# Product-key stage: the second parts of slabs, subkeys and query weights subtracted on VectorE instead of GpSimd

## Chip, cores and metric

One core of one Trainium2 chip. The metric is the device time of one execution in microseconds (us), the median of several runs. Engines are named as the profile names them: PE is TensorE (matmuls), PEld its weight loads, DVE is VectorE, ACT is ScalarE, POOL is GpSimd, SP is SyncE, which here only issues DMAs.

## What is computed

Two transformer blocks over 512 tokens of width 1024. The first has a latent attention, an indexed sparse attention and a mixture of experts; the second has three kinds of attention and then a product-key layer. All in float32. The change touches the product-key layer alone (and the slab products that are done ahead of it):

```python
def peer_ffn(h, w_q, subkeys, u, v):              # h: 512 tokens x 1024, already normed
    q = (hf @ w_q).reshape(T, 8, 2, 128)           # 8 heads, two halves of a key
    sc = jnp.einsum('thpd,hpkd->thpk', q, subkeys) # 128 scores per half
    s1, i1 = lax.top_k(sc[:, :, 0], 16)
    s2, i2 = lax.top_k(sc[:, :, 1], 16)
    # the 16 best sums s1 + s2 of each head choose 16 of 128 * 128 = 16384 experts
    top_s, pos = lax.top_k(cand, 16)
    gate = jax.nn.softmax(top_s, axis=-1)
    act = gelu(einsum('chkd,cd->chk', u[idx], h))  # a row of u and one of v for each expert
    out = einsum('chk,chkd->cd', gate * act, v[idx])
```

## The kernel before

**Two parts.** TensorE multiplies in a 32 bit format (fp32r) that drops low bits, so each operand is split: the first part is the rounded value, written by ACT (L185, `nc.scalar.copy`), the second is the rest, source minus first part (L187). `mm3` (L178 to L180) then takes three products in place of one. `split` puts the subtraction on DVE unless its argument `le` names another engine; `wunit` (L203) fetches a raw unit of 128x1024 values, splits it, and hands `le` on. In the tile names, `wr` is a raw unit, `wh` and `wl` are its two parts, and there are three buffers of each part and ten raw ones in this stage (`ring(10)`, L1761, nw=3).

**The product-key stage.** The matrix u is cut into 128 slabs of 128 experts. For 384 of the 512 tokens, `peer_s` (L1424) takes dense products of a slab with the normed tokens `hp` (24 matmuls of 128x384, then a gelu); for the first 128 tokens the rows of the chosen experts are gathered by indirect DMAs, which POOL issues (L1564), and DVE takes their dot products (L1569, tile `hy`) and later adds rows of v (L1567). In the order of the code:

- `peer_norm` (L1401) and `peer_early` (L1412), at the end of the stage before: norms, their transposes and splits (`hp`), and the products of slabs 0 and 1 (`ehl`).
- the subkeys (`sk`, two units) and the query weights (four chunks of four units, L1476): q, scores `s` and, on DVE, the 16 best of each half (`top16`, L1622 to L1626).
- `choose` for each of four tiles of 128 tokens, nearly all on DVE: the best sums and their keys, with five loops over 8 heads on 128x256 values (`big`, L1672, L1673, L1674, L1679, L1680) and three reductions (L1675, L1676, L1681). For tiles 1 to 3 PE then transposes the lists (L271, `t<-ident,i`).
- the matrix of gates: one-hot matrices on DVE (`ohA`, `ohB`, `ohE`, L1522 to L1525), multiplied on PE (L1530, L1531), copied by ACT into `stg`, stored and loaded again as `G`.
- slabs 2 to 71 (`s_step`, L1457, called at L1584), with one gather every second slab from the 24th on; then the main loop (L1592 on) over 128 slabs of v, 18 matmuls of 128x512 each, with the 56 slabs of u that are left (72 to 127) done eight steps ahead, and gathers at 1.3 a step.

**Order.** The engines run their queues in the order in which the program was laid down. That order isn't the order of the code: a planner (`schedule_with_timeline_sim`, L1852) lays it down when the program is built, from what it takes each instruction to last. So slabs run on PE beside the query, `choose` and the one-hot work, and a gather's dot product stands in DVE's queue in the midst of `choose`.

Of the kernel before, what the change touches and what calls it, by code (L numbers as in the profile page):

```python
# [20 lines left out]
P = 128  # L21
NT = 4
D = 1024
# [22 lines left out]
def staged(n, lag, first, then):  # L46
    """then(i, first(i)) for all i, first() running `lag` ahead"""
    r = {}
    for i in range(n + lag):
        if i < n:  # L50
            r[i] = first(i)
        if i >= lag:
            then(i - lag, r.pop(i - lag))


class Fill:
    """products kept in DRAM until the merge: sigmoids of gate columns, and output projections times those; 128
    columns at a time, feature-major.  They are queued in small pieces behind others whose results the tensor engine
    would wait for"""
# [7 lines left out]
    def gates(self, w, X, n0, n1, bias=None, raw=False):  # L67
        """gt[i] = tanh(z / 2) for the column tiles i = n0 .. n1 - 1 of z = (x @ W)^T + 2 bias; sigmoid(z) =
        (1 + tanh(z / 2)) / 2.  Without tanh and bias if raw"""
# [11 lines left out]
    def outs(self, w, X, g0, dst, prev=None, bias=None, raw=False):  # L81
        """dst[i] = 2 sigmoid(gate g0 + i) * (x @ W)^T of column tile i, + prev[i]"""
        nk = X[0].shape[1]
# [31 lines left out]
    def step(self, pool, after, n, end=False):  # L115
        """n row tiles, behind the instruction `after`; or those of the units that have begun (end)"""
# [23 lines left out]
    def rest(self, pool):  # L140
        """whatever is left"""
        while self.cur is not None or self.nxt is not None or self.jobs:
            self.step(pool, None, 1)


class Kernel:
# [12 lines left out]
    def ring(self, nr, nw=3):  # L159
        """the rings of weights: nr raw units as they arrive, nw units split into two parts"""  # L160
# [42 lines left out]
    def wunit(self, ap, nk, n, le=None, w=None, pool=None, after=None, cut=1):  # L203
        """one unit of weights: nk row tiles of n columns, split into two fp32r parts, in `cut` steps"""
# [9 lines left out]
    def proj_tok(self, XH, XL, units, nk, n, evac, nt=NT, cols=None, raws=(), le=None):  # L214
        """rows = tokens: psum[t] = x[t] @ W, W in units of row tiles"""
# [16 lines left out]
    def proj_tok1(self, XH, XL, units, nk, n, evac, follow=None, order=range(NT), pool=None):  # L232
        """proj_tok with all units on chip first: the tiles of tokens finish one after another; follow(t) comes behind
        the products of the next tile"""
# [16 lines left out]
    def proj_feat(self, XH, XL, units, nk, n, evac, ntok=512, le=None):  # L251
        """rows = output features: psum[c] = (x @ W[:, c])^T"""
# [15 lines left out]
    def T(self, out, src):  # L268
        """exact transpose"""
# [3 lines left out]
    def units(self, name, j, kn=2):  # L273
        """chunk j of a weight laid out [chunk, unit, partition, kn * n]"""
# [3 lines left out]
    def rstd(self, ss, n, pool=None, bufs=3):  # L278
        """1 / sqrt(ss / n + eps): first guess from the exponent bits, three Newton steps"""
# [26 lines left out]
    def to_feat(self, y, H, L, g=None, pool=None):  # L306
        """H, L [128, 8, 128] = parts of the transpose of y [128, 1024], times g [128, 8, 1]"""
# [16 lines left out]
    def norm_T(self, pool, src, g, HT=None, LT=None, nt=NT, keep=None):  # L324
        """rmsnorm(src(t)) * g into keep(t) if given, and the parts of its transpose into HT, LT [128, 8, nt * 128];
        src(t) -> [128, 1024]"""
# [11 lines left out]
    def rope(self, dst, src, nh, half, C, S):  # L338
        """dst, src [128, nh, >=2*half]; C = [c|c], S = [-s|s] of [128, 2*half]"""
# [10 lines left out]
    def transp(self, srcs, m, H, L, scale=None):  # L350
        """H, L [m, len(srcs) * 128] = parts of the transposes of srcs ([128, m] each)"""
# [5 lines left out]
    def softmax_rows(self, pool, s, n, bias=None, chunk_mask=False, np=NP):  # L357
        """P = softmax of the rows of psum s[:, :n]"""
# [21 lines left out]
    def block1_mix(self, cx, cm):  # L380
        nc, a = self.nc, self.a
        with ExitStack() as c0:
# [30 lines left out]
            with ExitStack() as c2:  # L413
# [5 lines left out]
                # keys for heads in the lower and upper 64 rows, zeros in the others: whole columns keep the clock up  # L419
# [74 lines left out]
                # latent attention  # L494
# [33 lines left out]
            with ExitStack() as c2:  # L528
# [6 lines left out]
                def behind(h, ins):  # L535
                    # the selection is needed later: one tile of queries per head
# [22 lines left out]
            # sparse attention  # L559
# [32 lines left out]
            # gated merge and output projection  # L592
# [1263 lines left out]
```

## Time and profile before

| | us |
|---|---|
| median of 3 runs | 2906.74 (2906.39 to 2907.47) |
| span of the profiled execution | 2904.9 |
| busy in that span: PE | 2735.4 (94%) |
| DVE | 2110.4 (73%) |
| ACT | 1283.6 (44%) |
| POOL | 1135.7 (39%) |

The span lies 1.84 us under the median of the runs. Shares over the whole span are means over stages; the product-key stage takes up about the last 1345 us. PE's busy time is modelled, and a matmul's record lasts longer than the distance to the next one, so the pace of matmuls is read from the distance between their starts.

### The profile page before, as it was taken

The numbers are of one execution on the slowest core, as the hardware profiler recorded it, in microseconds if no ns is written. First come the engines' busy times: TensorE is split into PE (matmuls) and PEld (weight loads), VectorE is DVE, ScalarE is ACT, GpSimd is POOL, SyncE is SP. The second block draws the span as 40 slices with busy tenths as digits, with TensorE's granted clock in tenths as the row PEclk, the third lists the DMA queues.
The fourth block names the chain that finished last, engine by engine and source line by source line (L and its number), as shares of the span: only waits on it lengthen the run. The fifth ranks groups of instructions, "written<-read, shape, count | busy, mean of one in ns | idle before, by whom it ended". The sixth has DMA issues, their size and how long they took to land.

```text
span 2904.9 us, 38412 instructions
## 1 busy us (share of the span) xinstructions
PE 2735.4 (94%) x13674; PEld 2353.4 (81%) x13674; DVE 2110.4 (73%) x4017; ACT 1283.6 (44%) x2021; POOL 1135.7 (39%) x682
## 2 busy tenths in 40 slices
PE   6999999789888999999998997899999999999999
PEld 5877777666666878798977897889988888888887
DVE  5758765798778464544475699999977788788885
ACT  3553443466665464533343232346643333333332
POOL 1120110465552231210122344554446565657661
PEclk9999999899999999999999998999999999999999
DMA  7222236688884332221353234567699999999994
GB/s 189 69 77 80 77 130 243 217 294 314 287 315 146 112 120 77 79 76 55 97 194 133 84 122 143 177 201 252 232 322 330 359 323 346 336 345 338 338 332 157
DMA packets 226774, 589.40 MB, mean 203 GB/s; under 512 B 25616, under 2 KB 90384, under 8 KB 224912
## 3 DMA queue, kind: packets, MB, share of 16 engines
q1 hardware_dynamic: 187408, 444.23, 44.3%
q0 software_dynamic: 39168, 142.65, 14.2%
q8 instruction: 110, 1.80, 0.2%
q14 instruction: 88, 0.72, 0.1%
HBM read 521.76 MB, written 65.04 MB: 202 GB/s over the span
## 4 chain that ended last, share of the span: by engine, by line
PE 62%; DVE 12%; issue 3%; POOL 2%; DMA 2%; ACT 1%; SPq 0%; POOLq 0%; DVEq 0%; ACTq 0%
PE acc L178 13%; PE acc L179 13%; PE acc L180 12%; PE s L178 4%; PE s L179 4%; PE s L180 4%; PE t L178 3%; PE t L180 3%; PE t L179 3%; DVE wl L187 2%; PE t L271 1%; DVE big L1672 1%; POOL wl L187 1%; DVE big L1680 1%; PE s L1530 1%
## 5 line engine op out<-in xcount | busy, mean ns | idle before, releaser
L187 POOL TENSOR_TENSOR wl<-wr,wh 128x1024 fp32r<-128x1024 f32 (+1 forms) x290 | 682.3, 2359 | 1139.0 <-ACT wh L185 1081.0
L185 ACT CAST wh<-wr 128x1024 fp32r<-128x1024 f32 (+3 forms) x637 | 622.3, 991 | 656.1 <-issue 298.9
L187 DVE TENSOR_TENSOR wl<-wr,wh 128x1024 fp32r<-128x1024 f32 (+3 forms) x347 | 493.1, 1428 | 181.8 <-ACT wh L185 177.9
L180 PE MATMUL acc<-hp,wl 128*128 128x384 f32 (+1 forms) x688 | 248.3, 361 | 6.4 <-POOL wl L187 6.4
L178 PE MATMUL acc<-hp,wh 128*128 128x384 f32 (+1 forms) x688 | 247.6, 361 | 0.0
L179 PE MATMUL acc<-hp,wh 128*128 128x384 f32 (+1 forms) x688 | 247.3, 359 | 0.0
L1564 POOL DMA_INDIRECT wr<-in_peer_u,idx x128 | 165.7, 1295 | 174.2 <-DVE dot L1569 59.2
L1564 POOL DMA_INDIRECT wr<-in_peer_v,idx x128 | 167.7, 1310 | 137.7 <-DVE x L1567 50.8
L1567 DVE SCALAR_TENSOR_TENSOR x<-wr,dot,x 128x1024 f32<-128x1024 f32 x128 | 195.7, 1529 | 26.3 <-DMA wr<-in_peer_v,idx 25.6
L185 ACT CAST WH<-act 128x384 fp32r<-128x384 f32 x128 | 65.8, 515 | 324.7 <-PE s L179 309.8
L1569 DVE CUSTOM_DVE_ANT_0 hy<-wr,gbc 128x1024 f32<-128x1024 f32 x128 | 184.4, 1440 | 23.4 <-DMA wr<-in_peer_u,idx 22.9
L179 PE MATMUL acc<-wl,WH 128*128 128x512 f32 x512 | 200.3, 391 | 0.0
L178 PE MATMUL acc<-wh,WH 128*128 128x512 f32 x512 | 197.4, 392 | 2.1 <-ACT WH L185 2.1
L180 PE MATMUL acc<-wh,WL 128*128 128x512 f32 x512 | 198.4, 389 | 0.0
L178 PE MATMUL t<-hp,wh 128*128 128x384 f32 x448 | 152.2, 340 | 0.0
L180 PE MATMUL t<-hp,wl 128*128 128x384 f32 x448 | 151.1, 337 | 0.8 <-POOL wl L187 0.8
L179 PE MATMUL t<-hp,wh 128*128 128x384 f32 x448 | 150.8, 337 | 0.0
L180 PEld LDWEIGHTS acc<-hp,wl 128*128 128x128 f32 x688 | 134.6, 196 | 11.9 <-POOL wl L187 6.8
L179 PEld LDWEIGHTS acc<-hp,wh 128*128 128x128 f32 x688 | 134.4, 195 | 5.3
L178 PEld LDWEIGHTS acc<-hp,wh 128*128 128x128 f32 x688 | 134.7, 196 | 4.8
L179 PE MATMUL s<-wl,XT 128*128 128x512 f32 x256 | 107.9, 421 | 27.3 <-DVE wl L187 24.8
L178 PEld LDWEIGHTS acc<-wh,WH 128*128 128x128 f32 x512 | 96.4, 188 | 20.5 <-ACT WH L185 2.4
(648 smaller groups left out, 7168.0 us busy)
## 6 DMA issues: line engine op xcount, KB each, us to landing
wr<-in_peer_vL SPq DMA_DIRECT2D x128, 512.0 KB
wr<-in_peer_uT SPq DMA_DIRECT2D x126, 512.0 KB
wr<-in_w_gu SPq DMA_DIRECT2D x122, 512.0 KB
wr<-in_w_dn SPq DMA_DIRECT2D x62, 512.0 KB
gd<-stg SPq DMA_DIRECT2D x12, 2048.0 KB
G<-gd SPq DMA_DIRECT2D x32, 768.0 KB
wr<-in_w_gate SPq DMA_DIRECT2D x24, 512.0 KB
act<-ad SPq DMA_DIRECT2D x56, 192.0 KB
```

Of the source, the lines that this page charges most:

```text
L178: mm(out, lh, rh, start=start, stop=False)
L179: mm(out, lh, rl, start=False, stop=False)
L180: return mm(out, ll, rh, start=False, stop=stop)
L185: nc.scalar.copy(H, src)
L187: return (le or nc.vector).tensor_tensor(L, src, H.bitcast(F32), op=ALU.subtract)
L271: self.nc.tensor.transpose(out, src, self.ident[:k, :k])
L1530: nc.tensor.matmul(o, A[:, b, :, ti], B[:, b, :, ti], start=True, stop=False)
L1564: nc.gpsimd.indirect_dma_start(out=row, out_offset=None, in_=a["peer_u" if f == "dot" else "peer_v"], in_offset=bass.IndirectOffsetOnAxis( ...
L1567: nc.vector.scalar_tensor_tensor(x[:, 0], row, dot0[:, e:e + 1], x[:, 0], op0=ALU.mult, op1=ALU.add)
L1569: nc.vector.tensor_tensor_reduce(scr, row, h0, 1.0, 0.0, ALU.mult, ALU.add, accum_out=dot0[:, e:e + 1])
L1672: tt(big[:, h], jc(posf), cb(self.poff[:, 0]), op=ALU.is_ge)
L1680: tt(big[:, h], big[:, h], d[:, h, 1][:, None, :].to_broadcast([P, 16, 16]), op=ALU.mult)
```

## The change

`split` is called without `le=nc.gpsimd` for the first two slabs, the subkeys, the query weights and all other slabs. The subtraction then goes to DVE. That is 2 + 2 + 16 + 126 = 146 instructions of 128x1024; nothing else that runs is altered (the rest of the diff takes out comments). POOL keeps the issue of the gathers here.

```diff
         for i in range(EARLY):
-            self.split(hl[:, i, 0], hl[:, i, 1], w[:, i, :D].rearrange("p (k n) -> p k n", k=8), le=nc.gpsimd)
+            self.split(hl[:, i, 0], hl[:, i, 1], w[:, i, :D].rearrange("p (k n) -> p k n", k=8))
             self.peer_s(hl[:, i, 0], hl[:, i, 1], w[:, i, D:], "acc", i)
...
             def s_step(k2, tag):
                 act[k2] = new_act()
-                uh, ul = self.wunit(a["peer_uT"][k2], 8, P, le=nc.gpsimd)
+                uh, ul = self.wunit(a["peer_uT"][k2], 8, P)
...
-                        self.split(sk[0][:, js], sk[1][:, js], w.rearrange("p (k n) -> p k n", k=8), le=nc.gpsimd)
+                        self.split(sk[0][:, js], sk[1][:, js], w.rearrange("p (k n) -> p k n", k=8))
...
                         self.proj_feat(HT, LT, self.units("w_peer_q_2", c), 8, 512,
-                                       lambda cc, ps: self.split(qT[0][:, cc], qT[1][:, cc], ps), le=nc.gpsimd)
+                                       lambda cc, ps: self.split(qT[0][:, cc], qT[1][:, cc], ps))
```

## Rows read from the trace of the kernel before

**Rows 1.** Chain that ended last (page, part 4): shares of the span by engine.

```profile
PE 62%; DVE 12%; issue 3%; POOL 2%; DMA 2%; ACT 1%; SPq 0%; POOLq 0%; DVEq 0%; ACTq 0%
```

**Rows 2.** Windows: stretch, its length, busy us and instructions by engine, granted clock, DMA.

```profile
1560.00:1582.00 22.00, 14.40 (x63) 12.98 (x62) 19.12 (x23) 7.90 (x11) 11.63 (x5) 0.69 0.73 286
1582.00:1758.00 176.00, 176.00 (x952) 159.03 (x951) 131.46 (x689) 51.98 (x67) 67.95 (x28) 1.00 0.33 104
1758.00:1919.00 161.00, 124.00 (x623) 121.82 (x622) 160.66 (x397) 45.56 (x61) 84.37 (x42) 0.86 0.54 166
1919.00:2120.00 201.00, 201.00 (x1391) 189.59 (x1390) 183.37 (x220) 132.29 (x149) 93.83 (x43) 1.00 0.67 238
...
2139.00:2888.00 749.00, 748.23 (x3593) 659.13 (x3594) 600.74 (x703) 265.64 (x368) 449.19 (x277) 1.00 0.92 327
```

**Rows 3.** Waits of PE, 1758 to 1919: waiter, releaser, total us, times, longest.

```profile
PE t L271 <- DVE i L1681: 15.0, 3, 6.1
PE t L271 <- DVE i L1675: 10.6, 2, 8.1
PE acc L180 <- POOL wl L187: 6.4, 1, 6.4
```

**Rows 4.** Timeline of PE at 1731 us: start, us, what.

```profile
1731.16 0.34 PE L180 MATMUL acc<-hp,wl 128*128 128x384 f32 x1
1731.34 0.34 PE L178 MATMUL acc<-hp,wh 128*128 128x384 f32 x1
```

**Rows 5.** Waits, 1560 to 1585: the longest of PE.

```profile
PE acc L179 <- DVE hp L187: 5.5, 1, 5.5
```

**Rows 6.** Line L187 on DVE: duration ns min/median/max, first and last start, forms.

```profile
L187 DVE TENSOR_TENSOR wl<-wr,wh x347: 544/1218/3426, 27.6 to 2889.6; 128x1024 fp32r<-128x1024 f32 x155, 128x768 fp32r<-128x768 f32 x14, 128x384 fp32r<-128x384 f32 x3, 128x720 fp32r<-128x720 f32 x2
```

**Rows 7.** Pieces of the chain, 1750 to 1812: start, us, what.

```profile
1755.09 2.34 DVE big L1680 x7
...
1797.06 1.14 DVE hy L1569
1798.21 7.62 DVE big L1680 x7
```

**Rows 8.** Timeline of POOL at two places.

```profile
1566.23 4.66 POOL L187 TENSOR_TENSOR sk<-wr,sk 128x1024 fp32r<-128x1024 f32 x2 [29.82 <-ACT sk L185]
...
1799.46 4.73 POOL L187 TENSOR_TENSOR wl<-wr,wh 128x1024 fp32r<-128x1024 f32 x2
```

**Rows 9.** Groups of DVE, 1695 to 1911: busy us, mean ns; `big` first and last of five.

```profile
L1672 DVE TENSOR_TENSOR big<-posf,poff 128x256 f32<-128x256 f32 x32 | 29.3, 977 | 0.1
...
L1569 DVE CUSTOM_DVE_ANT_0 hy<-wr,gbc 128x1024 f32<-128x1024 f32 x13 | 18.7, 1441 | 0.0
...
L1674 DVE TENSOR_TENSOR big<-big,poff 128x256 f32<-128x256 f32 x32 | 15.7, 544 | 0.0
```

**Rows 10.** Windows again: between two transposes of lists, and the stretch of `choose`.

```profile
1787.03:1840.65 53.62, 43.44 (x228) 42.84 (x229) 53.48 (x142) 16.98 (x22) 29.77 (x15) 0.91 0.61 181
...
1695.00:1911.00 216.00, 179.04 (x961) 176.86 (x959) 214.40 (x671) 67.85 (x90) 112.58 (x54) 0.91 0.51 158
```

**Rows 11.** Windows of line L187 on POOL alone: busy us and instructions.

```profile
1695.00:1758.00 63.00, 29.59 (x12) 1.00 0.44 141
1758.00:1919.00 161.00, 68.37 (x27) 0.86 0.54 166
```

**Rows 12.** Timeline of DVE, 1565 to 1579: the steps of a norm.

```profile
1566.23 2.37 DVE L289 SCALAR_TENSOR_TENSOR rs_t<-rs_y,rs_h 128x1 f32<-128x1 f32 x1
...
1577.90 0.16 DVE L293 SCALAR_TENSOR_TENSOR rs_y<-rs_t,rs_y 128x1 f32<-128x1 f32 x1
```

**Rows 13.** Groups of DVE, 1919 to 2120: one-hot lines, first and last of four.

```profile
L1525 DVE TENSOR_TENSOR ohE<-ohE,l_gl 128x1024 f16<-128x1024 f16 x48 | 53.8, 1137 | 0.3
...
L1522 DVE TENSOR_TENSOR ohA<-l_i,iok 128x1024 f16<-128x1024 f16 x45 | 36.9, 820 | 14.5 <-PE t L1531 14.3 <-issue 0.2
```

**Rows 14.** Line L1525: duration ns min/median/max.

```profile
L1525 DVE TENSOR_TENSOR ohE<-ohE,l_gl x48: 675/682/3293, 1923.1 to 2112.6; 128x1024 f16<-128x1024 f16 x48
```

## The prediction, as it was put on record

> **What bounds the kernel now.** I start with the chain that ended last: PE has 62% of it and DVE 12% [rows 1]. So the question is where in the product-key stage PE isn't the limit, and the windows answer it [rows 2]. From 1582 to 1758, from 1919 to 2120 and from 2139 to 2888 PE is busy all the time at full granted clock: what is taken off other engines there is worth nothing. Two stretches differ.
>
> *Stretch C, 1758 to 1919, is `choose`.* PE is busy 124 of 161 us at a mean granted clock of 0.86, and DVE 160.7 of 161. PE's waits there are nearly all for DVE: its transposes of the lists wait for the results of L1675 and L1681, and one slab waits 6.4 us for its subtraction on POOL [rows 3]. At full clock slab matmuls start 0.177 us apart (1731.16 to 1731.34, and so on) [rows 4], so the 623 matmuls of the window are 110 us of work and PE loses 51 us, 37 by waiting and some 14 by the lower clock behind each wait.
>
> *Stretch A, 1560 to 1582, is the end of the stage before.* 63 matmuls in 22 us at clock 0.69, again by the 0.177 us about 11 us lost; the longest wait is 5.5 us for the split of `hp` on DVE [rows 5].
>
> The ceiling of any gain is thus about 51 + 11.
>
> **What the subtraction costs on either engine.** On DVE one takes 1.22 us [rows 6], about 1.14 from start to start when they follow one another (the distance that the dot product of like size shows, [rows 7]); on POOL two take 4.73 us [rows 8]. But the row to read is another: in the chain, seven instructions of L1680 take 2.34 us at 1755, or 0.335 each, and the same seven take 7.62 us at 1798 [rows 7], while POOL runs two subtractions from 1799.46 on for 4.73 us [rows 8]. DVE stood still for 5.3 us. So an instruction of DVE with two inputs in SBUF and a subtraction on POOL don't overlap: the 2.4 us on POOL aren't beside DVE's work, they are taken out of it wherever DVE is at such a line. Moving one there costs 1.14 us and can free 2.4.
>
> **The Trainium skill** speaks against putting more on DVE here: its page Perfetto Trace Analysis, section "Optimizing Scalar/DVE Operations", says that where DVE is saturated it may pay to offload work, even to GpSimd, though it adds that the two share an SBUF read port and that it might not help between them. DVE is saturated in C, so the first half of the sentence would make the change a loss and the second half no gain; the 7.62 us against 2.34 us decide for the second here. What the first half alone would give stands below as a rival.
>
> **Stretch C, DVE's side.** The five `big` lines took 107.3 us for 160 instructions between 1695 and 1911 (L1672 is the first and L1674 the last of them in the table, [rows 9]); at 0.335 they are 53.6, so 53 us were blocks. I leave out smaller ones. DVE was busy 214.4 us of these 216 [rows 10]; without blocks and without its 13 dot products [rows 9] at 1.14 (15 us) 146 us remain. Added are 1.14 us a slab and, from the 24th slab on, a dot product every second slab. At full pace PE takes 24 x 0.177 = 4.25 us a slab, so with n slabs in a stretch of L us (6 us go to scores): L = 146 + 1.14 n + 0.57 (n - 22), n = (L - 6) / 4.25, which gives L = 220 and n = 50. Before, 12 + 27 = 39 subtractions of slabs fell in 1695 to 1919 [rows 11]. So DVE can feed PE at full pace through `choose`, which lasts about as long as now but holds 11 more slabs, 47 us of PE's work that the next stretch no longer has. That is the 51 us seen from the other side.
>
> Two things must hold. First, PE's transposes must stand in its queue where DVE's results come. Between two of them now stand 228 matmuls, 40 us at full pace, while they came 53.6 us apart [rows 10]; taking the blocks out of that interval (53 / 4 tiles = 13 us) leaves 40. The planned order thus fits a DVE that isn't blocked, and PE's waits are what the blocks add to it. Second, a slab's subtraction must not sit long in DVE's queue. The dot product at 1797.06 stands ahead of seven of the eight L1680 of its tile [rows 7], though those were ready: it seems that the planner's order takes what becomes ready first, not what is earlier in the code. With three pairs of buffers a subtraction is ready two slabs ahead of its use: 8.5 us, less cast and subtraction 6.2 us of slack.
>
> **Stretch A.** Five steps of a norm took from 1566.23 to 1577.90, 11.7 us [rows 12], against the two `sk` [rows 8] and three `wl` that POOL ran; unblocked such a step is 0.16 [rows 12], the five about 1. On DVE the five subtractions are 5 x 1.14 = 5.7. The gain is between 5 (all in front of the norm) and 10.7; I take 6, about PE's 5.5 us wait [rows 5]. The two `ehl` subtractions at 1531 fall where DVE is idle: nothing.
>
> **Stretch D, 1919 to 2120.** PE has 201 of 201 us to do and loses 47 of it: 154. DVE was busy 183 there; the four one-hot lines took 171 us for 186 instructions [rows 13], at the median of 0.682 [rows 14] 127, so 44 were blocks. 183 - 44 + 16 slabs x 1.14 - 5 dot products x 1.2 = 151 of 154. That is tight, and here lies what is late next: DVE at 98% beside a PE at 100%, each waiting on the other's order, won't keep pace exactly. I take 15 us of waits for C and D together; the bounds are 0 and 40 (then DVE's own load, not PE's, sets both).
>
> **The query, 1582 to 1758.** POOL's 28 subtractions x 1.14 = 32 us come to a DVE busy 131 of 176 [rows 2]. They fit, 93%; the cover is the lead of two units. Taken at 0; if they waited behind whole batches of `top16` it would cost up to 30, which the rival below takes in. **The main loop**: 56 x 1.14 = 64 on DVE's 601 of 749, even with no block removed 89%, and PE has no waits. Nothing. POOL keeps the gathers only; their subtractions no longer stand behind one that waits for `choose` (the 6.4 us, counted in C).
>
> **Sum**, against the span of 2904.9: 51 - 15 + 6 = 42 less, 2862.9; the runs lie 1.8 above the span: 2865.
>
> **The rivals.** (1) DVE becomes the bound of C and D: C takes its 220 us and D stays near DVE's present 183, because the one-hot lines also wait for PE (14.3 us [rows 13]) and get only part of their blocks back. Then 417 becomes 403, and with A 2906.7 - 14 - 6 = 2887. For it: the 98% worked out above. Against it: the median one-hot is 0.682.
> (2) The slower end: subtractions wait in DVE's queue behind `choose`. Each us of waiting beyond the 6.2 us of slack is a us of PE in each of the 50 slabs, so 0.9 us a slab beyond it eats the gain, and if `choose` goes first altogether (151 us from 1695 with some 5 slabs) the other 65 x 4.25 and the one-hot products (201 us less 623 slab matmuls of D at 0.177: 91) come after it: 1695 + 151 + 276 + 91 = 2213 against 2139 now, so about 2980. For it: `choose` comes first in the code. Against it: the dot product at 1797.
> (3) DVE's load only adds, no block is released: C and D gain nothing, 39 x 1.22 = 48 us come on top: 2955. Against it: the 7.62 us against 2.34 [rows 7]. The first half of the sentence of the Trainium skill (Perfetto Trace Analysis, as above) says this.
> (4) The change doesn't do what it says: the block stems from POOL's gathers, which stay, rather than from its subtractions; relief and added load about cancel: 2906. Against it: the 5.3 us lost at 1798 are as long as two subtractions [rows 8].
>
> **How the numbers follow.** Forecast 0.60, with 2846 to 2888 as its own range (waits of 0 to 38, A from 5 to 10.7); (1) 0.16; (2) 0.12, anywhere from 2910 to 2980; (3) 0.05; (4) 0.07. The range 2843 to 2907 takes in the forecast, (1) and half of (4), about 0.8. A measurement of this kernel tells some 0.2%, 6 us, from no change. Faster 0.60 + 0.16 = 0.76, with a little of (4) 0.77; same 0.06; slower 0.17.
>
> **What would show it.** In the profile after: L1672 to L1680 near 0.335 us each in a row (right) or still with means of 0.5 to 1 us (4); PE at full clock through `choose` with waits for L1675 and L1681 under 10 us; PE waits for `wl` of DVE of many us would be (2); D near 155 us (forecast) or 180 (1); the main loop unchanged at 749. The prediction is wrong if the planner, knowing that DVE is full, holds back the slabs, or if the query stage is no longer free of waits.

## The result and the profile of the kernel after

The kernel after takes **3006.42 us** (median of 4 runs, 3005.13 to 3020.32) against 2906.56 us for the kernel before in the same runs: ratio 1.0354, 95% interval 1.0332 to 1.0376. It is 100 us slower; 2865 was forecast, and the range ended at 2907. The profiled execution has a span of 3003.2 us (2904.9 before).

The chain that ended last, shares of the span by engine, kernel after (it answers [rows 1], where DMA has 2%):

```profile
PE 39%; DMA 20%; DVE 9%; issue 9%; POOL 2%; ACT 2%; SPq 0%; POOLq 0%; DVEq 0%; ACTq 0%
```

A fifth of the span is now waiting for transfers. The windows say where; kernel after, columns as in [rows 2] (stretch, length, busy us and instructions of PE, PEld, DVE, ACT, POOL, granted clock, DMA share, GB/s):

```profile
1560.00:1582.00 22.00, 18.82 (x107) 16.45 (x106) 17.27 (x36) 13.43 (x20) 0.00 (x0) 1.00 0.69 269
1582.00:1758.00 176.00, 176.00 (x951) 159.13 (x950) 151.16 (x717) 50.11 (x65) 0.00 (x0) 1.00 0.34 108
1758.00:1919.00 161.00, 156.95 (x883) 155.71 (x882) 147.48 (x424) 60.30 (x81) 32.47 (x20) 0.99 0.72 232
1919.00:2025.00 106.00, 106.00 (x685) 101.03 (x685) 88.75 (x136) 56.19 (x68) 19.44 (x16) 1.00 0.67 231
2025.00:2120.00 95.00, 67.06 (x520) 58.84 (x517) 82.85 (x134) 64.01 (x68) 4.94 (x4) 0.72 0.56 225
...
2139.00:2888.00 749.00, 684.40 (x3168) 589.16 (x3166) 524.84 (x657) 230.45 (x320) 262.11 (x203) 0.97 0.84 290
```

Read from top to bottom against [rows 2]. Stretch A has 107 matmuls for 63, the query stage stays full, and `choose` (1758 to 1919) has 883 matmuls for 623 at clock 0.99 for 0.86. On PE, up to 1919, the change does what was forecast. Then PE has no slab left: the last product of the 72 slabs that may run ahead of the main loop ends at 2024.2 us (2136.7 before), and from 2025 to 2120 PE holds 67 of 95 us at a mean clock of 0.72, between its two levels. And the main loop, "nothing" in the prediction, has 3168 matmuls in the 749 us that held 3593. From the start of its first product to that of its last it lasts 867.8 us (2130.6 to 2998.4); before, 761.3 us (2138.8 to 2900.1). The balance is complete: 8.2 us gained ahead of the loop, 106.5 lost in it, 98.3 in all, and the spans differ by 98.3.

What VectorE waits for in that loop; first the kernel before (waiter, releaser, total us, times, longest):

```profile
DVE WL L187 <- ACT WH L185: 51.0, 48, 3.5
DVE wl L187 <- ACT wh L185: 49.1, 33, 3.1
DVE x L1567 <- DMA wr<-in_peer_v,idx: 25.6, 22, 3.4
DVE hy L1569 <- DMA wr<-in_peer_u,idx: 17.5, 16, 2.2
```

and the kernel after, 2131 to 2998:

```profile
DVE x L1567 <- DMA wr<-in_peer_v,idx: 128.5, 81, 5.1
DVE hy L1569 <- DMA wr<-in_peer_u,idx: 107.8, 54, 4.6
DVE WL L187 <- ACT WH L185: 11.7, 8, 1.9
```

The waits for gathered rows grew from 43 to 236 us. DVE is busy for 598 us of this loop: with its waits it is full, and PE waits for it. PE in the same stretch of the kernel after (before, it waited 2.9 us in all):

```profile
PE acc L179 <- DVE wl L187: 51.9, 30, 3.9
PE t L180 <- DVE wl L187: 21.1, 14, 3.3
PE acc L178 <- ACT WH L185: 13.7, 1, 13.7
```

Two rows may be put side by side, POOL's issues and DVE's dot products (timelines of the kernel after; start, us, engine, line, operation; in brackets the idle time before it and what ended it). POOL:

```profile
2497.01 1.02 POOL L1564 DMA_INDIRECT wr<-in_peer_u,idx  x1 [4.12 <-DVE dot L1569]
2499.66 1.69 POOL L1564 DMA_INDIRECT wr<-in_peer_u,idx  x1 [1.63 <-DVE dot L1569]
```

DVE:

```profile
2501.37 1.22 DVE L1569 CUSTOM_DVE_ANT_0 hy<-wr,gbc 128x1024 f32<-128x1024 f32 x1 [0.84 <-DMA wr<-in_peer_u,idx]
...
2506.21 1.23 DVE L1569 CUSTOM_DVE_ANT_0 hy<-wr,gbc 128x1024 f32<-128x1024 f32 x1 [2.01 <-DMA wr<-in_peer_u,idx]
```

Rows are used in the order in which they are issued, so the issue that ended at 2498.03 belongs to the dot product at 2501.37, and that of 2501.35 to the one at 2506.21: 3.3 and 4.9 us from the end of the issue to the landing. DVE does 2.5 and 2.8 us of other work in between, and then it stands, with the slabs' subtractions behind it. Call the time from the end of a row's issue to the start of its use its *lead*. Its median from 2250 us on is 7.5 us in the kernel before and 5.4 us in the kernel after. Where DVE waits, the wait is part of the lead. DVE's own work between the end of an issue and the use, which holds no waiting, has a median of 6.0 us in the loop of the kernel before and 3.1 us in that of the kernel after. (The Trainium skill, DMA: Bandwidth & Descriptors, section "Anatomy of one DMA — SWDGE (gpsimd) path", fits 2.0 us plus the bytes at 436 GB/s for such a transfer: for the 512 KB of a row tile that is an estimate of 3.2 us. The first of the two pairs agrees; the median lead, in a loop that moves 290 GB/s in all, is longer.)

### The profile page after: what moved, and what is told of

Same layout as the page of the kernel before. It is cut to its first block, busy times and chain, and to the rows that moved or that the text cites. A ratio compares the mean times of both kernels' runs of the same rounds, so it can differ in the third digit from the quotient of the medians.

```text
span 3003.2 us, 38429 instructions
## 1 busy us (share of the span) xinstructions
PE 2760.7 (92%) x13674; PEld 2355.1 (78%) x13674; DVE 2087.9 (70%) x4163; ACT 1279.7 (43%) x2021; POOL 754.7 (25%) x536
## 4 chain that ended last, share of the span: by engine, by line
PE 39%; DMA 20%; DVE 9%; issue 9%; POOL 2%; ACT 2%; SPq 0%; POOLq 0%; DVEq 0%; ACTq 0%
PE acc L178 10%; PE acc L179 10%; PE acc L180 10%; DMA wr<-in_peer_v,idx 9%; DMA wr<-in_peer_u,idx 7%; DVE wl L187 4%; PE s L178 2%; PE s L179 2%; PE s L180 2%; POOL wr L1564 2%; DMA wr<-in_w_dn 1%; PE t L271 1%; ACT wh L185 1%; DMA wr<-in_peer_vL 1%; DMA act<-ad 1%
## 5 line engine op out<-in xcount | busy, mean ns | idle before, releaser
L187 DVE TENSOR_TENSOR wl<-wr,wh 128x1024 fp32r<-128x1024 f32 (+3 forms) x489 | 656.4, 1348 | 158.7 <-ACT wh L185 152.1
L187 POOL TENSOR_TENSOR wl<-wr,wh 128x1024 fp32r<-128x1024 f32 (+1 forms) x148 | 303.5, 2061 | 891.2 <-ACT wh L185 854.1
L1564 POOL DMA_INDIRECT wr<-in_peer_u,idx x128 | 166.7, 1302 | 804.5 <-DVE t L1624 269.7
L179 PE MATMUL acc<-wl,WH 128*128 128x512 f32 x512 | 211.4, 413 | 52.1 <-DVE wl L187 51.9
L1567 DVE SCALAR_TENSOR_TENSOR x<-wr,dot,x 128x1024 f32<-128x1024 f32 x128 | 164.4, 1284 | 129.2 <-DMA wr<-in_peer_v,idx 128.5
L1564 POOL DMA_INDIRECT wr<-in_peer_v,idx x128 | 173.4, 1354 | 293.9 <-DVE x L1567 187.2
L180 PE MATMUL acc<-hp,wl 128*128 128x384 f32 (+1 forms) x688 | 240.4, 352 | 4.0 <-DVE wl L187 4.0
L1569 DVE CUSTOM_DVE_ANT_0 hy<-wr,gbc 128x1024 f32<-128x1024 f32 x128 | 156.4, 1222 | 123.5 <-DMA wr<-in_peer_u,idx 123.2
L179 PE MATMUL acc<-hp,wh 128*128 128x384 f32 (+1 forms) x688 | 242.2, 352 | 0.0
L178 PE MATMUL acc<-hp,wh 128*128 128x384 f32 (+1 forms) x688 | 241.5, 352 | 0.2 <-ACT hp L185 0.2
L178 PE MATMUL acc<-wh,WH 128*128 128x512 f32 x512 | 206.5, 403 | 13.7 <-ACT WH L185 13.7
L179 PEld LDWEIGHTS acc<-wl,WH 128*128 128x128 f32 x512 | 100.2, 196 | 84.8 <-DVE wl L187 66.2
L178 PEld LDWEIGHTS acc<-hp,wh 128*128 128x128 f32 x688 | 130.0, 189 | 5.4 <-ACT hp L185 0.5
L179 PEld LDWEIGHTS acc<-hp,wh 128*128 128x128 f32 x688 | 130.3, 189 | 4.8
```

The costliest lines, as they stand in the source:

```text
L178: mm(out, lh, rh, start=start, stop=False)
L179: mm(out, lh, rl, start=False, stop=False)
L180: return mm(out, ll, rh, start=False, stop=stop)
L187: return (le or nc.vector).tensor_tensor(L, src, H.bitcast(F32), op=ALU.subtract)
L1564: nc.gpsimd.indirect_dma_start(out=row, out_offset=None, in_=a["peer_u" if f == "dot" else "peer_v"], in_offset=bass.IndirectOffsetOnAxis( ...
L1567: nc.vector.scalar_tensor_tensor(x[:, 0], row, dot0[:, e:e + 1], x[:, 0], op0=ALU.mult, op1=ALU.add)
```

## The experiments

The question is what shortens the lead. All 56 subtractions that the change brings into the loop lie on DVE, so the loop's own load was the first suspect; the state in which the loop is entered was the rival. One table for the runs in which rows and weights share a ring of buffers as in the two kernels; the others follow in the text. "Loop" is from its first product to its last. "Waits" are DVE's for rows in the loop. "Head start" is how many rows that belong to steps of the loop (not to the slabs ahead of it) are used before the loop's first product. "Lead" is the median from 2250 us on. "Held" is the mean number of rows issued and not yet used up, over the same stretch; the ring has ten buffers for rows and weights together (eight in x11). The last three are counted from the issues of L1564 on POOL and the starts of the dot products and adds on DVE.

| kernel | time, us | loop | waits | head start | lead | held |
|---|---|---|---|---|---|---|
| before | 2907 | 761 | 43 | 8 | 7.5 | 3.4 |
| x2_main_dve | 2907.6 | 761 | 15 | 8 | 9.1 | 3.6 |
| x15_all_but_slabs | 2904.7 | 762 | 90 | 9 | 6.7 | 3.1 |
| x13_before_hold | 2903.9 | 759 | 4 | 0 | 9.3 | 3.9 |
| x11_before_ring8 | 2897.4 | 759 | 35 | 6 | 8.0 | 3.4 |
| x7_hold_start | 2890.2 | 761 | 2 | 2 | 10.5 | 4.2 |
| x4_later | 2883.6 | 761 | 0 | 2 | 16.4 | 6.1 |
| after | 3006.4 | 868 | 236 | 15 | 5.4 | 2.2 |
| x1_main_pool | 2970.7 | 830 | 184 | 15 | 5.2 | 2.4 |
| x14_early_dve | 2963.6 | 832 | 178 | 15 | 5.3 | 2.4 |
| x12_before_spill40 (loop has 68 us more to do) | 3025.7 | 908 | 193 | 15 | 5.2 | 2.3 |
| x8_spill64 (loop has 34 us less to do) | 2976.2 | 823 | 214 | 15 | 5.3 | 2.2 |

### The loop's own subtractions: x2_main_dve and x1_main_pool

```diff
 x2_main_dve, in the kernel before:
-                uh, ul = self.wunit(a["peer_uT"][k2], 8, P, le=nc.gpsimd)
+                uh, ul = self.wunit(a["peer_uT"][k2], 8, P, le=None if k2 >= SPILL + HOLD else nc.gpsimd)
 x1_main_pool, in the kernel after:
-                uh, ul = self.wunit(a["peer_uT"][k2], 8, P)
+                uh, ul = self.wunit(a["peer_uT"][k2], 8, P, le=nc.gpsimd if k2 >= SPILL + HOLD else None)
```

> The kernel before, with only the 56 slabs of the main loop subtracted on VectorE. Lead and work both expect the loop at 850 to 860 and the whole at 2906.6 + 107 = 3014, the first stages as before. The rival (the state in which the plan enters the loop) expects 2907.

> The changed kernel, but the 56 slabs of the main loop (72 to 127) are subtracted on GpSimd again; the other 90 instructions stay on VectorE. The time went in the main loop (856 us after, 749 before), while the stretch up to its start is 8 us shorter. Both theories of the main loop (lead: the dot products and adds of gathered rows stand too close behind their gathers in VectorE's queue; work: VectorE has 56 subtractions more) expect the loop at about 750 and the whole at 2906.6 - 8 = 2898. If instead the loop's order was spoilt by what comes ahead of it (a rival: the plan merely starts from another state), the loop stays near 856 and the whole near 3000.

x2_main_dve took 2907.62 us, ratio 1.0002 (0.9991 to 1.0012). Its window of the loop, 2139 to 2888:

```profile
2139.00:2888.00 749.00, 749.00 (x3596) 659.81 (x3596) 608.28 (x757) 265.17 (x368) 278.61 (x221) 1.00 0.92 326
```

POOL has 171 us less to do there, DVE's waits for rows fell to 15 us, and PE has all 749 us: 56 subtractions in the loop cost nothing. x1_main_pool took 2970.71 us, ratio 1.0213 (1.0188 to 1.0237):

```profile
2139.00:2888.00 749.00, 703.76 (x3298) 605.97 (x3298) 568.52 (x640) 240.39 (x333) 409.24 (x264) 0.99 0.86 304
```

With the loop written as in the kernel before, it still loses 69 us. So the loop's own load isn't the cause, and what is done ahead of it is. Only where DVE is already full by its waits do the 56 subtractions count: 3006.4 - 2970.7 = 36 us. The traces of these two runs also hold the landings of the rows, counted here from the start of an issue; first x2_main_dve, then x1_main_pool, over their loops:

```profile
DMA to landing us min/median/max: 4.5/7.1/9.7
DMA to landing us min/median/max: 4.3/5.8/10.8
```

From the end of the issue that is a median of 5.8 us in x2 (3.1 to 8.6) and of 4.5 us in x1 (3.2 to 8.1). So the rows don't land later in the slow loop; they are used sooner after their issue.

### Which part ahead of the loop: x14_early_dve and x15_all_but_slabs

```diff
 x14_early_dve, in the kernel before:
-                uh, ul = self.wunit(a["peer_uT"][k2], 8, P, le=nc.gpsimd)
+                uh, ul = self.wunit(a["peer_uT"][k2], 8, P, le=None if k2 < SPILL + HOLD else nc.gpsimd)
 x15_all_but_slabs, in the kernel after:
-                uh, ul = self.wunit(a["peer_uT"][k2], 8, P)
+                uh, ul = self.wunit(a["peer_uT"][k2], 8, P, le=nc.gpsimd)
```

> The kernel before with one part of the change alone: slabs up to the 72nd (those ahead of the main loop) subtracted on VectorE; the slabs of the main loop, subkeys and query weights stay on GpSimd. Theory 'the slabs ahead of the loop do it': they run out some 90 us early as in the kernel after, rows are used 3.6 steps ahead or more, loop 825 to 870, time 2965 to 3010. Rival 'the free GpSimd of the query stage does it': loop 761, choose without blocks, time 2885 to 2905.

> The kernel after with all slabs subtracted on GpSimd again; subkeys, query weights and the two early slabs' ehl stay on VectorE. Theory 'the slabs ahead of the loop do it': choose is blocked as in the kernel before, no lull, loop 761, only the end of the stage before gains its 4 to 6 us: time 2900 to 2907. Rival 'the query stage does it': rows used 3.6 steps ahead or more, loop 825 or more, time 2965 or more.

x14_early_dve took 2963.62 us, ratio 1.0193 (1.0164 to 1.0222). DVE's waits in its loop:

```profile
DVE x L1567 <- DMA wr<-in_peer_v,idx: 101.0, 53, 6.3
DVE hy L1569 <- DMA wr<-in_peer_u,idx: 77.1, 47, 4.0
```

x15_all_but_slabs took 2904.66 us, ratio 0.9997 (0.9980 to 1.0013), with a loop of 762 us, although DVE waits 90 us for rows there: so much still fits into its idle time. Without the subtractions of the slabs ahead of the loop there is no loss, and alone they bring 57 of the 100 us; most of the rest are the 36 us that the loop's own subtractions cost once the waits are there. In x14 as in the kernel after, `choose` runs without blocks and the slabs run out at 2024 us.

### Is it the lull? x12_before_spill40 and x8_spill64

```diff
 x12_before_spill40, in the kernel before; x8_spill64 in the kernel after has 64:
-SPILL, ND, EARLY = 56, 384, 2
+SPILL, ND, EARLY = 40, 384, 2
```

> The kernel before with 40 instead of 56 slabs whose scores are kept in DRAM, so 56 instead of 72 slabs may run ahead of the main loop: subtractions stay on GpSimd, but PE runs out of slabs some 68 us earlier (16 x 4.25), and the loop has 68 us more to do (829 us without waits). Theory 'the lull': a lull before the loop is by itself what lets the rows run ahead; then rows are used about 4 steps ahead, DVE waits for them 150 us or more in the loop, loop 890 to 935, time 3010 to 3080. Rival 'the lull is not enough': use stays near 2.9 steps ahead, row waits stay near the 43 us of the kernel before, loop 825 to 840, time 2945 to 2980.

> The kernel after with 64 instead of 56 slabs whose scores are kept in DRAM, so 80 instead of 72 slabs may run ahead of the main loop. PE runs out of slabs some 34 us later (8 x 4.25), the lull before the loop shrinks from about 92 to 58 us, and the loop has 34 us less to do (727 instead of 761 without waits). Theory 'head start': with a shorter lull rows are used less far ahead and part of the 106 us that the loop lost comes back: time 2870 to 2950, loop 730 to 800. Rival 'the plan within the loop': its losses stay at about 106 us: loop about 833, time about 2972. Rival 'DVE is full': the one-hots become slower beside a busy PE and the slabs gain nothing: time about 3006.

x12_before_spill40 took 3025.74 us, ratio 1.0412 (1.0389 to 1.0435). No subtraction was moved; `choose` is as blocked as before, but the slabs run out at 2019 us. Its windows:

```profile
1758.00:1919.00 161.00, 123.57 (x626) 121.36 (x625) 160.66 (x405) 44.81 (x60) 83.78 (x42) 0.86 0.54 164
...
2025.00:2120.00 95.00, 61.19 (x427) 53.03 (x428) 74.36 (x126) 52.34 (x58) 3.88 (x4) 0.66 0.65 241
```

DVE's waits in its loop:

```profile
DVE x L1567 <- DMA wr<-in_peer_v,idx: 103.4, 72, 6.1
DVE hy L1569 <- DMA wr<-in_peer_u,idx: 89.3, 49, 4.8
```

PE's lull from 2025 to 2120 is there, and so are 193 us of waits and a loop of 908 us where 761 + 68 = 829 are work. A lull ahead of the loop is enough by itself; the engine of the subtractions isn't needed. x8_spill64 makes the lull shorter (slabs until 2086, one-hots until 2144) and took 2976.22 us, ratio 1.0234 (1.0217 to 1.0251): its loop loses 96 us, as the rival had it. My expectation that a shorter lull does less harm fell. The head start says why: it is 15 rows in all five kernels with a loss, whatever the length of the lull, so it fills up to a limit and stays there. The rows in flight show the limit: when the slabs end, these five have used 9 or 10 rows of the loop and issued 11; in the lull they use up all 15 that are issued, and the loop begins with none under way. The kernel before begins it with 3 (11 issued, 8 used).

### Holding back the first uses: x4_later, x7_hold_start, x13_before_hold

```diff
+            self.last = self.split(h[:, s], l[:, s], w[:, s], le=le, after=after)
 ...
             def gathers(r):
+                if late[0]:
+                    use(self.last)
                 credit[0] += r
                 ...
+                    held.append((f, e, row))
+                if not late[0]:
+                    use(None)
+
+            def use(behind):
+                while held:
+                    f, e, row = held.pop(0)
+                    with self.tc.issue_after(behind.ins) if behind is not None else ExitStack():
+                        ... dot product or add, as before
 ...
             load_g(blocks[0])
+            late[0] = True
 ...
+                late[0] = n < 12
```

x4_later holds all rows of the stage in this way, x7_hold_start and x13_before_hold (the same edit in the kernel before) only those of the first twelve steps.

> The changed kernel with one thing more: the dot product or add of a gathered row is laid down one call of the gathering function later and queued behind the subtraction that was laid down last before it, so more of VectorE's work stands between a gather and its use. Lead expects more than 6 us of VectorE's work between the two (4.0 after, 6.8 before), waits for rows well under 100 us and the loop under 790, the whole 2895 to 2930. Work expects no change, about 3005.

> The kernel after, but for the gathers of the first twelve steps of the main loop (and of the slabs prepared ahead of it) the dot product or add is laid down one call of gathers() later and queued behind the last subtraction; from the thirteenth step on everything is as in the kernel after. In the traces so far a row of the main loop is issued 4.7 to 4.9 steps of the loop ahead of its slab's product in every kernel, but used 2.9 steps ahead in the kernel before, 4.1 in the kernel after and 3.6 in x1_main_pool. Theory 'head start': the used-ahead figure is carried through the loop from the moment at which it is entered (the slabs run out some 90 us early, the dots run ahead in that lull), so a hold over twelve steps alone restores it: used ahead near 3 for the rest, loop 760 to 775 us instead of 868, time 2895 to 2915. Rival 'the plan within the loop': the order goes back to 4 steps ahead as soon as the hold ends, whatever the entry was: loop 840 to 868, time 2975 to 3006.

> The kernel before with the hold of x7_hold_start (gathers of the first twelve steps of the loop used one call later), subtractions on GpSimd. It tells what of the 17 us by which x7_hold_start beats the kernel before belongs to the change of engine and what to the hold. If the hold only takes away a disturbance that the kernel before doesn't have: loop 761, time 2902 to 2912, and the change of engine is worth about 17 us once the loop is left alone. If the hold is a gain of its own: 2890 or less, and the change is worth nothing.

x4_later took 2883.59 us, ratio 0.9923 (0.9906 to 0.9939); x7_hold_start 2890.16 us, ratio 0.9941 (0.9925 to 0.9958); both lie under the kernel before, by 0.8 and 0.6%, although in them, too, the slabs run out early, at 2026 and 2039 us. In x7, steps 13 to 127 are written as in the kernel after. DVE's waits in its loop:

```profile
DVE wl L187 <- ACT wh L185: 66.6, 104, 2.7
DVE WL L187 <- ACT WH L185: 61.5, 74, 2.0
DVE x L1627 <- PE acc L180: 6.5, 1, 6.5
DVE hy L1579 <- DMA wr<-in_peer_u,idx: 2.0, 2, 1.1
```

236 us of waits for rows are 2, and around step 105, ninety steps after the hold, the lead is still 10.5 us. This is what tells history from load: the loop keeps nearly to the end a distance that was set at its entry (x7 begins it with 6 rows under way). x13_before_hold took 2903.88 us, ratio 0.9994 (0.9984 to 1.0005): where there is no lull the hold is worth nothing. So the 17 us by which x7 beats the kernel before are the change's own, and they are made ahead of the loop: x7's begins at 2122.0 us, 16.8 earlier.

### The ring of buffers: x11, x3, x17, x16, x19

Why does the distance last? A row's buffer comes free with its use, and the next row or weight takes it: rows that are used early hold few buffers, 2.2 of ten in the kernel after, while weights fetched ahead hold 7.7 (3.4 and 6.4 before). These runs ask whether this split carries the loss.

```diff
 x11_before_ring8:  -    k.ring(10)   +    k.ring(8)
 x3_nowait, in the kernel after (rows go to two buffers that nobody reads):
+                    row = pgz.tile([P, D], F32, name="gz", tag="gz", bufs=2)
-                    nc.vector.tensor_tensor_reduce(scr, row, h0, ...
+                    nc.vector.tensor_tensor_reduce(scr, h0, h0, ...
 ...                  (the add reads h0 in place of row, too)
 x16_after_rows4 (x17_before_rows2: bufs=2 and k.ring(8), in the kernel before):
-                    row = self.raw()
+                    row = self.rw.tile([P, D], F32, name="wr", tag="gr", bufs=4)
-    k.ring(10)
+    k.ring(6)
 x19_rows4_step, on top of x16:
+                    with self.tc.issue_after(self.loaded.ins):
                         nc.gpsimd.indirect_dma_start(out=row, ...
```

> The kernel before with a ring of 8 instead of 10 raw buffers in the product-key stage, nothing else. Weights and gathered rows share the ring in the order of the code, about 3.3 allocations a step of the main loop, so two buffers fewer let a row be issued about 0.6 steps (3.6 us) later. Theory 'ring and distance': issued ahead falls from 4.7 to about 4.1 steps, the lead between issue and use from 7.6 us to 4 to 5, DVE waits for rows as in the kernel after (200 us and more instead of 50), loop 800 to 870 us, time 2950 to 3010. Rival: the lead is set by the planned order alone and uses move back with the issues: loop 761, time 2900 to 2915.

> The changed kernel, in which the gathers still move their rows, into two buffers that nobody reads, and the dot products and adds of VectorE read a tile that is on chip all the time; the gathered part of the layer is thus left out, with every instruction of VectorE still there. Lead expects the waits of VectorE for rows (236 us in the loop) gone and the loop at 750 to 765, the whole about 2900. Work expects the loop still at about 850, the whole near 3000, since VectorE's load is the same.

> The kernel before, with two raw buffers for gathered rows and eight for weights instead of ten for both: no lull, subtractions on GpSimd. It puts the split of the kernel after into the kernel before. Theory: some 217 rows of the loop have two buffers, each held for about 8 us (1.0 to 1.7 issue, 5.2 to landing, 1.2 use): 4 us a row, loop 850 to 930, time 2990 to 3080. Rival (the number of buffers for rows isn't what the loop lacks): loop 761 to 780, time 2900 to 2930.

> The kernel after, with the ten raw buffers of the stage divided by hand: four of their own for gathered rows, six for weights; engines, order of the code and memory stay the same, and nothing is held back. Counted in the traces so far (issued, not yet used), rows hold 3.4 and weights 6.4 of the ten in the loop of the kernel before, 2.2 and 7.7 in the kernel after; loops with 3.1 rows or more lose nothing, loops with 2.4 or less lose 69 to 106 us. Theory 'weights keep the buffers that they took in the lull': with four of their own, rows hold up to 4 whatever the entry was: row waits under 50 us, loop 758 to 770, time 2883 to 2900 in spite of the lull. Rival 'the planned order of the uses alone' (rows are laid down too early on VectorE, whichever buffer they have): waits of 200 us, loop 830 to 868, time 2965 to 3006.

> x16_after_rows4 (four raw buffers for rows, six for weights) with each gather planned behind the last weight fetch that stands ahead of it in the code, so that rows can't run further ahead of the slabs than six weights. In x16 the loop lost nothing (760.4 us), but 80 rows were used ahead of the loop that the kernel after uses in it, and choose and the one-hots waited for them; so that run doesn't tell whether four buffers or the smaller number of rows mended the loop. Theory 'the split of the buffers': with rows kept in step the loop has its 210 rows or more, row waits stay under 50 us, loop 758 to 770; choose is as in the kernel after (one-hots from about 1950): time 2883 to 2900. Rival 'the planned order alone': waits of 150 us or more, loop 830 to 868, time 2960 to 3006. If rows still run ahead of choose: loop 760 and 2960 as in x16, and nothing is told.

x11_before_ring8: 2897.44 us, ratio 0.9967 (0.9956 to 0.9977). My expectation fell: with two buffers fewer the weights gave them up (4.4 for 6.4), rows still hold 3.4, and the lead is 8.0 us. Eight buffers or ten make no loss here, so the size of the ring alone isn't the limit.

x3_nowait took 3164.2 us, ratio 1.0884 (1.0854 to 1.0913), its loop 762 us. This loop says nothing about the waits, since it has no row to use: dot products and adds that wait for no row are laid down ahead of and among `choose` and the one-hots, and the last of all 256 starts at 2315.9 us, before the loop's first product at 2332.5 (L1568 is the add here; number, duration in ns min/median/max, first and last start):

```profile
L1568 DVE SCALAR_TENSOR_TENSOR x<-gbc,dot,x x128: 1242/1349/1468, 1918.9 to 2315.9; 128x1024 f32<-128x1024 f32 x128
```

A window of what comes ahead of the loop:

```profile
2025.00:2120.00 95.00, 30.46 (x170) 29.46 (x169) 94.57 (x223) 15.59 (x21) 1.19 (x1) 0.68 0.15 47
```

and two of PE's waits, 1700 to 2340:

```profile
PE t L271 <- DVE i L1676: 37.9, 1, 37.9
PE t L271 <- DVE i L1682: 31.1, 2, 15.7
```

DVE is full and PE waits for the lists.

x17_before_rows2: 3007.93 us, ratio 1.0333 (1.0309 to 1.0357), 221 us of row waits and a loop of 802 us that uses 191 rows (224 in the kernel before). Two buffers for rows bring the waits into the kernel before, as the theory had it, but the loop stays under the 850 us expected, since rows left it and 60 us of the loss lie ahead of it (it begins at 2198.9 us). x16_after_rows4: 2963.86 us, ratio 1.0195 (1.0178 to 1.0212). Its loop is the forecast 760 us without row waits, but it uses only 137 rows (217 in the kernel after); the others went ahead, among and before the one-hots, as in x3. So it is the shared ring that keeps the rows in step with the slabs. The longest of PE's waits from 1560 on:

```profile
PE s L1530 <- DVE ohB L1524: 44.7, 22, 3.5
PE acc L178 <- ACT WH L185: 23.5, 1, 23.5
PE s L1531 <- DVE ohE L1525: 20.0, 24, 4.8
```

The 137 rows are not spread thinner: they fill the first 72 steps of the loop with 32 rows per 100 us, as many as in the kernel before (31), and none is waited for. A head start of 95 rows does that loop no harm; it is entered with 4 rows under way. That speaks for the buffers; but the order of the uses is another one, too, so it doesn't decide. x19_rows4_step was to keep the rows in step and didn't (2965.41 us, ratio 1.0197, again 137 rows). So it is shown that a short lead, once there, lasts, and that two buffers for rows are too few; whether the weights' hold on the buffers is what makes it last, or the order of uses alone, stays open.

### Does it pay with the loop mended and more slabs? x9_later_spill64

> x4_later with 64 instead of 56 slabs kept in DRAM: rows are used late as there, and PE gets 34 us more of slabs into the lull before the main loop. If the prediction's reading of that stretch holds (PE's work is what counts there) the time is 2883.6 - 34 = 2850, between 2845 and 2862. If DVE's one-hots set that stretch and grow longer beside a busy PE, 2870 to 2884. If row waits return, over 2900.

x4_later with `SPILL` 64 took 2873.71 us, ratio 0.9882 (0.9865 to 0.9898), the fastest here. The loop gave its 34 us (727 for 761), but the one-hots end at 2127 us for 2098, so 10 us are left by the medians (5 between the profiled executions); the expected 2850 fell, and the time is that of its second case. The same step on top of x16 and x19 (x18_rows4_spill64 and x20_rows4_step_spill64) gave 2953.61 and 2955.20 us, 10 us each, with a loop of 727 us in x18; they tell nothing more.

> x16_after_rows4 with 64 instead of 56 slabs kept in DRAM. If the split of the buffers is the cause, the loop has 34 us less to do and loses nothing: loop 725 to 735; the stage ahead of it grows as it did between x4_later and x9_later_spill64 (some 24 us), so 7 to 13 us less than x16_after_rows4: 2870 to 2893. Rival: loop 800 or more as in x8_spill64, time 2950 to 2980.

> The same with 64 instead of 56 slabs kept in DRAM. Theory 'the split of the buffers': loop 725 to 735, time 7 to 13 us below x19: 2870 to 2893. Rival: loop 800 or more, over 2950.

## Why the prediction was wrong, step by step

**The blocks: right.** The groups of DVE from 1700 to 1919, kernel after (busy us, mean ns), answer [rows 9]:

```profile
L1569 DVE CUSTOM_DVE_ANT_0 hy<-wr,gbc 128x1024 f32<-128x1024 f32 x19 | 23.2, 1221 | 13.1 <-DMA wr<-in_peer_u,idx 13.1
...
L1674 DVE TENSOR_TENSOR big<-big,poff 128x256 f32<-128x256 f32 x32 | 11.7, 414 | 0.0
L1672 DVE TENSOR_TENSOR big<-posf,poff 128x256 f32<-128x256 f32 x32 | 11.5, 418 | 0.1
...
L1675 DVE TENSOR_REDUCE i<-big 128x128 f32<-128x2048 f32 x4 | 9.1, 2274 | 0.0
```

L1672 takes 418 ns for 977, while L1675, with one input, has the same 2.27 us (median) in both kernels. The timeline of the same kernel has eight L1680 in 2.75 us, where [rows 7] has seven in 7.62:

```profile
1754.43 2.75 DVE L1680 TENSOR_TENSOR big<-big,dix 128x256 f32<-128x256 f32 x8
```

and L1525 (minimum, median, maximum ns; [rows 14] has a maximum of 3293):

```profile
L1525 DVE TENSOR_TENSOR ohE<-ohE,l_gl x48: 676/684/692, 1944.0 to 2112.7; 128x1024 f16<-128x1024 f16 x48
```

Rivals (3) and (4) fall. The Trainium skill, SBUF — State Buffer, section "Who interferes with whom", says that a VectorE instruction with two inputs in SBUF contends with a GpSimd instruction that reads SBUF, and that the port pair which they share is an exclusive lock; these rows agree. The offloading hint of the Trainium skill that the prediction weighed (Perfetto Trace Analysis, "Optimizing Scalar/DVE Operations") would have kept the blocks here; its second half, that the shared port may spoil it, is the one that applies.

**Stretch A and the query: right but for a little.** A was 6, with 5 as its lower bound; the first query product starts at 1581.3 for 1585.3 us, 4 earlier (8.7 in x15). The query stage has PE busy 176 of 176 us with all subtractions on DVE.

**Stretch C: right on PE, short on DVE.** 260 more matmuls in 1758 to 1919 are 46 us of work at 0.177; 51 was forecast. PE's only wait in it is 4.0 us for a slab's subtraction on DVE, so rival (2) as it was put falls too. 50 subtractions of weights ran on DVE from 1700 to 1919, and n = 50 was worked out. But `choose` did not last "about as long as now": DVE's first one-hot starts at 1935.1 for 1914.3 us, 21 later. Waiting for rows had no term in L, and DVE waited 13.1 us for them (the line of L1569 above; none before); dot products more than the 14 worked out account for most of the rest (21 from 1695 to 1935).

**Stretch D: a step that failed.** "PE has 201 of 201 us to do and loses 47 of it: 154" treats PE's work as what sets the end. The work was indeed done earlier, but nothing stood in its place: the kernel lets 72 slabs run ahead of the loop, and the loop's own slabs come behind the one-hots. The 47 us turned into PE's idle time. The end is set by the one-hots, mainly on DVE, for which 151 us were worked out and which was busy 171.6 of 201: 20 dot products came where 12 (five fewer than before) were assumed, 19 subtractions instead of 16, and the last `choose` slipped past 1919 (PE's one-hot products begin at 1946.2 for 1925.3 us). PE's longest waits from 2024 to 2131, of which the kernel before has only the first, with 2.1 us:

```profile
PE acc L178 <- ACT WH L185: 13.7, 1, 13.7
PE s L1531 <- DVE ohE L1525: 12.2, 11, 2.6
PE s L1530 <- DVE ohB L1524: 10.1, 9, 1.6
```

The first of them are the 14 us in which nothing covers the load of `G`; before, slabs did. Of 42 us, 8 arrived by the loop's first product.

**The main loop: the step that decided.** "... even with no block removed 89%, and PE has no waits. Nothing." The sum of the load was right, as x2 shows: 56 subtractions there cost nothing. What failed is that a stage in which nothing costs anything was taken to be independent of how it is entered. The warning stood in the trace of the kernel before, in waits that the prediction does not use: DVE's for rows, 43 us. They showed that some rows landed only just in time, and that cover, unlike a share of busy time, can be lost without adding a single instruction. The lull did it: every row that was issued was used before the loop began (15 ahead instead of 8), the lead fell from 7.5 to 5.4 us, and 236 us of waits filled the idle time that 89% had promised. Why a short lead stays short through the loop remains open.

**The rivals.** Ahead of the loop, rival (1), DVE as the bound of C and D, comes nearest: it gave 20 us there, and 8 came. The slower side was given 0.17 and mainly one mechanism, subtractions queued behind `choose`, up to 2980. Subtractions did queue behind something on DVE, but behind waits for rows, in another stage, and the time lies beyond the 2980. Had the loop stayed as it was, the change would have been worth what x7 and x13 say: 2890 against 2904, 14 to 17 us rather than 42.

## What to carry to other kernels

Where a stage has slack, ask what the slack is made of: an engine's idle time, or the distance between a transfer's issue and its use. The second depends on how the stage is entered and can vanish in a stage whose own instructions aren't the cause, so read the waits of the engines that aren't the bound, too. And before work that is pulled forward is counted as a gain, look for the limit on how far it may run ahead (here 72 slabs) and for what the engine does when it is reached.

## What the runs showed of the hardware that was not expected

A gathered tile of 128 rows of 4 KB landed 3.3 and 4.9 us after the end of its issue in the two pairs shown. Over whole loops, where the trace has the landings, it took 3.1 to 8.6 us with a median of 5.8 (x2, 326 GB/s in its window) and 3.2 to 8.1 us with a median of 4.5 (x1, 304 GB/s). A lead near the median is thus too short: with 5.2 to 5.4 us, in five kernels, DVE waits 178 to 236 us; with 6.7 us (x15) it waits 90 us and the loop loses nothing; with 10.5 us (x7) it waits 2 us.

An instruction with two inputs of 128x256 float32 values (L1672) took 418 ns on DVE without GpSimd's subtractions and 977 ns on average among them; a reduction with one input (L1675) took 2.27 us either way.
